# Keys and two values ahead of the score folds: a new order for the weight folding that opens a decoder trunk

## Chip, cores and metric

The kernel runs on one core of a Trainium2 chip. The metric is the device time of one execution in microseconds; the time before is 2403.75 us, the median of three runs (2400.74 to 2407.68).

## What is computed

One layer of a hybrid decoder trunk on x (2048 tokens x 1024 channels, f32) and a memory of 256 tokens, then a final norm:

```
mem_n = rmsnorm(mem, mem_norm_g)
h = rmsnorm(x, mix_norm_g);  q, k, v, g, u = split(h @ w_in)
y_ret  = silu(g) * head_rmsnorm(retention(rope(q), rope(k), v))
y_pool = pool_mixer(u, pool_w) * pool_scale
x = x + concat(y_ret, y_pool) @ w_out
K, V = split(mem_n @ wkv)                 # 4 heads of 256 channels, 256 tokens
x = x + softmax((rmsnorm(x) @ wq) @ K.T / 16) @ V @ wo
x = x + ffn(rmsnorm(x))                   # gated, causal convolution of width 3
out = rmsnorm(x, final_norm_g)
```

The memory has only 256 tokens, so the kernel folds weights before it touches x: `wq` with the keys (a score matrix per head), the values with `wo`, and `pool_w` with the pool's rows of `w_out`. These folds and the norm statistics of the first half of x make up the opening, the first 119 us or so. The change lies there.

## The kernel before

**Numbers.** f32 operands are split in two f32r parts, high (ACT, L264, or L267 with a gain) and low (DVE, L248 or L256), and each product is three matmuls: high x high, high x low, low x high (`passes`, L276 to L278). A weight tile of 128 x 1024 costs one DMA of 512 KB, one ACT pass and one DVE pass before PE can use it.

**The steps of the opening** (`folded_weights`, L430) are traced in the order of the table at L622:

- K 0 to 7 (`keys`, L521) and V 0 to 7 (`memory_values`, L535) each load one tile of `wkv` and project the memory with it (`project`, L499): 8 blocks of 128 channels x 3 passes = 24 matmuls of 256 columns. Two tiles share one PSUM bank. After every second V the bank is split into the value parts (`parted`, L509). A key bank must first be multiplied by the memory's inverse root mean square (`scaled_keys`, L514).
- That scale comes from `memory_norm` (L487), called behind the third key tile: squares on ACT, sums on DVE, four small matmuls over the partitions (`stats`, L350, L357), three Newton steps on DVE for the reciprocal root (`rsqrt`, L300), then `spread` (L365): DVE multiplies an identity by the two parts of the result, PE multiplies by ones (L381), and ACT copies the product to SBUF (L386), so that each column holds its token's scale.
- M 0 to 3 (`score_weights`, L551) fold two rows of `wqT` with two key parts: 4 banks x 2 columns x 2 rows x 3 passes = 48 matmuls; ACT evicts and its queue writes `Md`.
- O 0 to 3 (`output_weights`, L572) fold two rows of `wo` with the values into `VWd`; W 0 to 3 (`pool_weights`, L600) fold the pool weights into `WPd`. Their matmuls have 512 columns.

**Beside them** the loop at L2086 counts the steps n and places the eight tiles of x (`load_x_wide`, L647: load, split, square, add to `total`), the statistics of x (`rows_norm`, L2007, at n = 21, behind O2) and the four loads of value weights (`value_weights`, L726), which the `values` stage reads afterwards.

**What sets the order.** Instructions are traced in program order; a planner with a timing model then orders each engine's queue, the earlier traced first among those that it takes to be ready. `keep_in_program_order` pins an instruction behind the one traced before it on its engine; `issue_after(ins)` pins what its block traces on ins's engine behind ins. On the chip each queue runs strictly in its order. PE has five PSUM banks named `mm`.

**Places.** Raw weights land in a ring of nine places of 512 KB (`raws`, L2083: three in R, two in S, four in Z); a load takes the place that was left longest ago and waits until its last reader is done. `total` holds one such place (R) until `rows_norm` frees it, and memory two until the statistics have read them. Split weights go round a ring of five places (`wides`, L439: Q, two in E, two in G). `other_places` (L441) exchanges two of them behind M3 for the keys' region and four behind V7 for the memory's. SP issues all the loads in one queue.

Of the kernel before, what the change touches and what calls it, by code (L numbers as in the profile page):

```python
# [20 lines left out]
NMEM = 256  # L21
# [121 lines left out]
def trunk(ctx, tc, xT, memT, pos, w_qkgu, w_v, wkv, wqT, wo, wout_r, wout_p, poolT, w_up, w_dn, vecs, consts, outT):  # L143
    nc = tc.nc
    pe, act, dve, pool, sp = nc.tensor, nc.scalar, nc.vector, nc.gpsimd, nc.sync
# [14 lines left out]
    def new_e(at, dtype):  # L160
        return Arena(cp.tile([P, 2 * T], dtype, tag=f"E{at}", name=nm("E")), 0, 2, T)
# [14 lines left out]
    raws = Places([(R, j * T) for j in range(3)] + [(r, 0) for r in S], T)  # L176
# [41 lines left out]
    ones = cp.tile([P, P], F32R, tag="ones", name="ones")  # L218
# [19 lines left out]
    def aux():  # L238
        if both[0] and next(turns_) % 3 == 2:
            return single()  # L240
        return auxp.tile([P, SUB], F32, tag="aux", name=nm("aux"))

    def small(n=4):
        t = smp.tile([P, 8], F32, tag="sm", name=nm("sm"))
        return t[:, :n]

    def tt(eng, out, a, b, op):
        return eng.tensor_tensor(out=out, in0=a, in1=b, op=op)  # L248
# [9 lines left out]
    def bcast(v, n):  # L258
        return v.rearrange("p (a o) -> p a o", o=1).to_broadcast([P, v.shape[1], n])
# [20 lines left out]
    def new_raw():  # L280
        r = raws.take()
        r.free()
        return r.f
# [30 lines left out]
    behind, under, fetched = [iter(())], [iter(())], [None]  # L314
    turned, chained = [], []
    latest, summed = [None], [None]
# [33 lines left out]
    def stats(sums, more=None):  # L350


        cols = [ap[:, t * P : (t + 1) * P] for ap in sums for t in range(ap.shape[1] // P)]
        n = len(cols)
        ps = aux()
        for t, ap in enumerate(cols):
            pe.matmul(ps[:, t : t + 1], ap, one, start=True, stop=more is None)  # L357
            if more is not None:
                pe.matmul(ps[:, t : t + 1], more[:, t * P : (t + 1) * P], one, start=False, stop=True)
        v, y = small(n), small(n)  # L360
        ts(dve, v, ps[:, :n], 1.0 / D, ALU.mult, EPS, ALU.add)
        rsqrt(y, v)
        return y

    def spread(y, outs, keep=True, late=False):  # L365

        yh = smp.tile([P, 8], F32R, tag="yh", name=nm("yh"), bufs=1)[:, : y.shape[1]]
        yl = small(y.shape[1])
        dve.tensor_copy(yh, y)
        tt(dve, yl, y, yh.bitcast(F32), ALU.subtract)  # L370
        at = 0

        one_pair = prs.take() if late else None
        for out in outs:
            n = out.shape[1] // P
            d = one_pair if late else B.take()
            ps = aux()[:, : n * P]
            for i, v in enumerate((yh.bitcast(F32), yl)):
                di = d.r[:, i * SUB : i * SUB + n * P]
                last = tt(dve, di.rearrange("p (a b) -> p a b", a=n), ident.rearrange("p (o b) -> p o b", o=1).to_broadcast([P, n, P]), bcast(v[:, at : at + n], P), ALU.mult)  # L380
                pe.matmul(ps, ones, di, start=i == 0, stop=i == 1)  # L381
            if d is not one_pair or out is outs[-1]:
                d.free()
            if not keep:
                return ps
            act.activation(out, ps, AF.Copy)  # L386
            at += n
        return last
# [41 lines left out]
    def folded_weights():  # L430
# [51 lines left out]
                split(first[:, at], u0[0][:, at], u0[1][:, at], kept="both")  # L482
        rm = TT.take()
        rn = smp.tile([P, 4], F32, tag="rnm", name="rnm", bufs=1)[:, :2]
        bank = []

        def memory_norm():  # L487
            for r in memory:
                tc.keep_in_program_order(act.activation(r.f, r.f, AF.Square))
            f, other = (r.f for r in memory)  # L490
            tt(dve, f, f, other, ALU.add)
            for w in (SUB, NMEM):
                tt(dve, f[:, :w], f[:, :w], f[:, w : 2 * w], ALU.add)
            dve.tensor_copy(rn, stats([f[:, :NMEM]]))
            for r in memory:
                r.free()
            spread(rn, [rm.f[:, :NMEM]], late=True)

        def project(n):  # L499

            u = u0 if n == 0 else wide_pair(second, 2) if n == 1 else wide_pair(load_tile(wkv[n]))
            if n % 2 == 0:
                bank[:] = [mmps()]
            at = n % 2 * NMEM
            ps = bank[0][:, at : at + NMEM]
            for k in range(KT):
                passes(ps, [r[:, k * P : (k + 1) * P] for r in u], (mh[:, k], ml[:, k]), k == 0, k == KT - 1)

        def parted(to, n, ps):  # L509

            hi, lo = (to[:, n - 1 : n + 1, i] for i in range(2))
            split(ps.rearrange("p (n m) -> p n m", n=2), hi, lo)

        def scaled_keys(n, ps):  # L514

            ps3 = ps.rearrange("p (n m) -> p n m", n=2)
            both = rm.f[:, :NMEM].rearrange("p (o m) -> p o m", o=1).to_broadcast([P, 2, NMEM])
            tt(dve, ps3, ps3, both, ALU.mult)
            parted(kp4, n, ps)

        def keys(n):  # L521

            early = bank[0] if n == 2 else None
            project(n)
            if n == 1:
                sp.dma_start(cs_t, consts)
            elif n == 2:
                memory_norm()
                scaled_keys(1, early)
            elif n % 2:  # L530
                scaled_keys(n, bank[0])
            if n == KT - 1:
                rm.free()

        def memory_values(n):  # L535
# [53 lines left out]
        def pool_factors():  # L589

            raw = TT.take()
            r3 = raw.f[:, :SUB].rearrange("p (g c) -> p g c", g=4)
            sp.dma_start(r3, poolT.rearrange("g p c -> p g c"))
            pw = prs.take()
            tt(dve, r3, r3, bcast(pscale, P), ALU.mult)
            split(raw.f[:, :SUB], pw.r[:, :SUB], pw.r[:, SUB:])
            raw.free()
            pool_pair.append(pw)
# [17 lines left out]
        def none_left():  # L616
            mp.free()
            for r in own:
                r.free()

        K, V, M, O, W = keys, memory_values, score_weights, output_weights, pool_weights
        for f, *a in ((K, 0), (K, 1), (K, 2), (K, 3), (K, 4), (K, 5), (M, 0), (K, 6), (M, 1), (K, 7), (V, 0), (M, 2), (V, 1), (V, 2),  # L622
                      (M, 3), (V, 3), (O, 0), (V, 4), (V, 5), (O, 1), (V, 6), (O, 2), (V, 7), (W, 0), (W, 1), (O, 3), (W, 2), (W, 3),
                      (none_left,)):
            f(*a)
            if f is M and a[0] == 3:
                pool_factors()
            yield
# [97 lines left out]
    def value_weights(kp, where=None):  # L726
        raw = new_raw()
        sp.dma_start(raw.rearrange("p (k n) -> p k n", k=2), w_v[2 * kp : 2 * kp + 2].rearrange("k p n -> p k n"))
        u = (B if where is None else B.arenas[where]).take(2)
        for i in range(2):  # L730
            r = raw[:, i * SUB : (i + 1) * SUB]
            split(r, u.r[:, i * T : i * T + SUB], u.r[:, i * T + SUB : (i + 1) * T])
        return u
# [1273 lines left out]
    def rows_norm(s_acc):  # L2007
        rn = smp.tile([P, 8], F32, tag="rn", name=nm("rn"), bufs=3)
        dve.tensor_copy(rn, stats([r.f[:, : r.f.shape[1] // SUB * SUB] for r in s_acc]))
        for r in s_acc:  # L2010
            r.free()
        return rn
# [69 lines left out]
    under[0], spacing[0] = weight_sums(), 2  # L2082
    raws = Places([(R, j * T) for j in range(3)] + [(r, 0) for r in S] + [(Z.arenas[0].t, j * T) for j in range(4)], T)  # L2083
    results = Places([(Z.arenas[1].t, j * T) for j in range(4)], T)
    wv, total, x_at = [], raws.take(), (5, 7, 9, 10, 12, 13, 15, 18)
    for n, _ in enumerate(folded_weights()):  # L2086
        if n in x_at:
            load_x_wide(x_at.index(n), total)
        if n == 21:
            rn = rows_norm([total])  # L2090
        if n in (23, 24):
            wv.append(value_weights(len(wv), 0))
        if n in (25, 26):
            wv.append(value_weights(len(wv), len(wv) - 1))
    rb = [TT.take() for _ in range(NS)]
    normed = (rn, rb)
    behind[0] = spread_steps(rn, [r.f[:, :SUB] for r in rb])
# [1 line left out]
    for b in range(NB):  # L2099

        if b == 0:
            raws = Places([(R, j * T) for j in range(3)] + [(r, 0) for r in S], T)
# [123 lines left out]
        wv, acc, place = [], [], Joined(new_e(0, F32), new_e(1, F32))  # L2226
# [105 lines left out]
    raws = Places([(raws.one[i].t, raws.one[i].base + j * SUB) for i in raws.freed for j in range(2)], SUB)  # L2332
# [116 lines left out]
```

## Time and profile before

| | |
|---|---|
| median of three runs | 2403.75 us |
| the profiled execution | 2400.9 us (span 2399.1, clock 0.996) |
| PE busy, matmuls | 2372.3 us, 11136 |
| DVE, ACT busy | 1796.7, 1386.3 us |
| DMA over the span | 527.78 MB, mean 220 GB/s |
| DMA, on queue q1 | 402.83 MB |

In the profile PE is the matmul engine and PEld its weight loads; DVE, ACT, POOL and SP are the other engines, and a q behind a name is that engine's queue. "L381 <- DVE Q" says that the instruction of line 381 waited for DVE to write tile Q. A helper's line stands for all its callers (L248 is every two-operand DVE operation), so the tiles tell them apart. Matmuls overlap, so the distance between two starts, not the duration, is what one costs. The views by stages give busy time in a stretch, and beside it the clock that TensorE was granted, where 1.00 is full.

### The profile page before, as it was taken

The page shows a single profiled execution, that of the slowest core. Times are in us where ns is not written, and L with a number is a line of the kernel's source. Part 1 is how long each engine was busy: PE and PEld are TensorE (multiplying, and loading weights), DVE is VectorE, ACT ScalarE, POOL GpSimd, SP SyncE. Part 2 cuts the span into 40 slices and gives each one's busy share as a digit, 9 for nine tenths or more (in the row PEclk, how much of TensorE's full clock was granted, in tenths as well). Part 3 has the DMA queues.
Part 4 walks back from the last instruction along what each step waited for, and adds up shares of the span by engine and source line. Part 5 has one row for each costly group of instructions (what it writes and reads, how often), then busy time and mean ns, then how long its engine had stood idle before and what let it go on. Part 6 is the DMA issues. An engine that isn't in the chain of part 4 may idle for free.

```text
span 2399.1 us, 33436 instructions
## 1 busy us (share of the span) xinstructions
PE 2372.3 (99%) x11136; PEld 1981.9 (83%) x11136; DVE 1796.7 (75%) x2977; ACT 1386.3 (58%) x2507; POOL 340.6 (14%) x524
## 2 busy tenths in 40 slices
PE   8999999999999999999999999999999999999998
PEld 7888888888888888888888888888888888888886
DVE  6777776785767777776788776987677698867875
ACT  6754654564445545546555555855555577666663
POOL 0055554454041000000001000110000000000000
PEclk9999999999999999999999999999999999999999
DMA  8899999999585234577578564765456489768951
GB/s 292 303 277 302 283 266 290 297 291 315 191 234 142 74 116 151 172 251 243 168 229 264 180 188 133 254 201 174 157 174 190 132 258 313 237 184 283 342 176 73
DMA packets 269453, 527.78 MB, mean 220 GB/s; under 512 B 30048, under 2 KB 50912, under 8 KB 269280
## 3 DMA queue, kind: packets, MB, share of 16 engines
q1 hardware_dynamic: 212176, 402.83, 51.1%
q0 software_dynamic: 40960, 94.40, 16.5%
q10 hardware_dynamic: 16144, 28.43, 3.2%
q8 instruction: 87, 1.43, 0.2%
q14 instruction: 86, 0.70, 0.1%
HBM read 423.30 MB, written 196.61 MB: 258 GB/s over the span
## 4 chain that ended last, share of the span: by engine, by line
PE 92%; DMA 3%; DVE 3%; ACT 1%; issue 1%; SPq 0%; ACTq 0%; DVEq 0%
PE mm L276 28%; PE mm L278 28%; PE mm L277 28%; PE aux L276 1%; PE aux L278 1%; PE aux L277 1%; PE aux L799 1%; PE aux L773 1%; PE aux L784 1%; PE aux L946 1%; PE aux L801 1%; PE aux L357 0%; DMA WPd<-Z 0%; DVE Z L248 0%; DMA S<-w_v 0%
## 5 line engine op out<-in xcount | busy, mean ns | idle before, releaser
L276 PE MATMUL mm<-G,Q 128*128 128x512 f32 (+1 forms) x1445 | 559.0, 388 | 1.8 <-ACT T L1788 0.5
L277 PE MATMUL mm<-G,Q 128*128 128x512 f32 (+1 forms) x1445 | 558.7, 387 | 0.2 <-DVE G L256 0.2
L278 PE MATMUL mm<-G,Q 128*128 128x512 f32 (+1 forms) x1445 | 555.9, 387 | 1.0 <-DVE Q L248 1.0
L277 PE MATMUL mm<-G,E 128*128 128x512 f32 (+1 forms) x1072 | 410.4, 383 | 1.6 <-DVE G L248 1.6
L276 PE MATMUL mm<-G,E 128*128 128x512 f32 (+1 forms) x1072 | 409.2, 383 | 2.7 <-ACT G L264 2.3
L278 PE MATMUL mm<-G,E 128*128 128x512 f32 (+1 forms) x1072 | 408.9, 383 | 0.4 <-DVE E L248 0.2
L276 PEld LDWEIGHTS mm<-G,Q 128*128 128x128 f32 x1445 | 271.5, 188 | 57.6 <-ACT T L1788 1.0
L278 PEld LDWEIGHTS mm<-G,Q 128*128 128x128 f32 x1445 | 271.5, 188 | 55.4 <-DVE Q L248 1.4
L277 PEld LDWEIGHTS mm<-G,Q 128*128 128x128 f32 x1445 | 271.7, 188 | 54.1 <-DVE G L256 0.4
L248 DVE TENSOR_TENSOR Z<-Z,mm 128x512 f32<-128x512 f32 (+1 forms) x290 | 193.6, 672 | 91.6 <-PE mm L278 89.4
L256 DVE SCALAR_TENSOR_TENSOR Z<-Z,vecs,Z 128x1024 f32<-128x1024 f32 x176 | 224.7, 1280 | 50.1 <-ACT Z L1218 45.5
L276 PEld LDWEIGHTS mm<-G,E 128*128 128x128 f32 x1072 | 202.2, 189 | 42.8 <-ACT G L264 2.6
L277 PEld LDWEIGHTS mm<-G,E 128*128 128x128 f32 x1072 | 202.3, 189 | 40.8 <-DVE G L248 1.9
L278 PEld LDWEIGHTS mm<-G,E 128*128 128x128 f32 x1072 | 202.3, 189 | 40.1 <-DVE E L248 1.0
L248 DVE TENSOR_TENSOR Q<-R,Q 128x512 fp32r<-128x512 f32 (+2 forms) x205 | 140.1, 684 | 81.9 <-ACT Q L1155 48.4
L248 DVE TENSOR_TENSOR T<-T 128x512 f32<-128x512 f32 (+4 forms) x196 | 134.0, 690 | 26.4 <-ACT T L423 12.4
L1155 ACT ACTIVATE Q<-R 128x512 fp32r<-128x512 f32 (+1 forms) x123 | 75.7, 616 | 128.5 <-PE mm L277 119.9
L1155 ACT ACTIVATE E<-R 128x512 fp32r<-128x512 f32 (+1 forms) x163 | 100.3, 615 | 70.9 <-PE mm L277 56.1
L1218 ACT ACTIVATE Z<-Z,vecs 128x1024 f32<-128x1024 f32 x88 | 109.2, 1242 | 37.8 <-DVE Z L248 36.9
L1102 ACT ACTIVATE G<-T 128x512 fp32r<-128x512 f32 x180 | 108.2, 623 | 32.7 <-DMA T<-Gd 24.3
L248 DVE TENSOR_TENSOR Q<-S,Q 128x512 fp32r<-128x512 f32 (+2 forms) x113 | 77.1, 683 | 39.9 <-ACT Q L1155 30.1
L1155 ACT ACTIVATE Q<-S 128x512 fp32r<-128x512 f32 (+1 forms) x81 | 49.9, 616 | 95.5 <-PE mm L277 93.7
(425 smaller groups left out, 4428.9 us busy)
## 6 DMA issues: line engine op xcount, KB each, us to landing
T<-Gd SPq DMA_DIRECT2D x168, 256.0 KB, 4.4
Ud<-w_up POOLq DMA_DIRECT2D x132, 256.0 KB, 9.7
Gd<-Z SPq DMA_DIRECT2D x110, 256.0 KB, 2.7
R<-Ud SPq DMA_DIRECT2D x104, 256.0 KB, 2.7
R<-w_up SPq DMA_DIRECT2D x82, 256.0 KB, 2.9
S<-Ud SPq DMA_DIRECT2D x72, 256.0 KB, 2.8
Gd<-T SPq DMA_DIRECT2D x56, 256.0 KB, 3.4
T<-Xd SPq DMA_DIRECT2D x53, 256.0 KB, 4.4
```

What stands on the lines that cost most here:

```text
L248: return eng.tensor_tensor(out=out, in0=a, in1=b, op=op)
L256: return dve.scalar_tensor_tensor(out=out, in0=a, scalar=s, in1=b, op0=op0, op1=op1)
L276: pe.matmul(ps, lh, rh, start=start, stop=False, skip_group_check=more)
L277: pe.matmul(ps, lh, rl, start=False, stop=False, skip_group_check=more)
L278: latest[0] = pe.matmul(ps, ll, rh, start=False, stop=stop, skip_group_check=more)
L773: pe.matmul(col(sc, c), self.ch(k, c), self.ch(q, c), start=True, stop=True)
L784: pe.matmul(col(kv, c), col(self.kn.f, c), self.ch(v, c, h * T), start=True, stop=True)
L799: pe.matmul(col(y, c), col(self.pr.f, c), self.ch(v, c, h * T), start=True, stop=self.cur[c] is None)
L801: pe.matmul(col(y, c), self.ch(q, c), self.cur[c], start=False, stop=True)
L1102: one = act.activation(hi, x, AF.Copy, scale=-1.0 if i == 2 else 1.0)
L1155: act.activation(p2[:, 0, :w], self.raw[i].f[:, :w], AF.Copy)
L1218: act.activation(self.c[g].f, a[:, 2:], AF.Identity, bias=cb[:, f : f + 1], scale=cw[2][:, f : f + 1])
```

## The change

1. The table of steps: K6 and K7 come directly behind K5, then V0 and V1, and from there score folds alternate with values (M0, V2, M1, V3, M2, V4, M3). Before, M0 and M1 stood between K5, K6 and K7, and M2 behind V0.
2. `memory_norm` still runs behind K2 but no longer spreads its result. The spread moves behind the last key, its two matmuls pinned behind the last matmul of K7 (`behind`), and all four key banks are scaled there instead of each behind its second tile.
3. The steps at which x's tiles and the value weights are placed change with the table. The last two value weights now come together behind W3.
4. `total.back = None`: when the sum of x's squares is freed, its place does not go back into the ring of raw places.

```diff
-    def spread(y, outs, keep=True, late=False):
+    def spread(y, outs, keep=True, late=False, behind=None):
...
-                pe.matmul(ps, ones, di, start=i == 0, stop=i == 1)
+                with tc.issue_after(behind) if behind is not None else nullcontext():
+                    pe.matmul(ps, ones, di, start=i == 0, stop=i == 1)
...
-        bank = []
+        bank, done = [], []
...
-            spread(rn, [rm.f[:, :NMEM]], late=True)
...
-            early = bank[0] if n == 2 else None
             project(n)
             if n == 1:
                 sp.dma_start(cs_t, consts)
             elif n == 2:
                 memory_norm()
-                scaled_keys(1, early)
-            elif n % 2:
-                scaled_keys(n, bank[0])
+            if n % 2:
+                done.append((n, bank[0]))
             if n == KT - 1:
+                spread(rn, [rm.f[:, :NMEM]], late=True, behind=latest[0].ins)
+                for pair in done:
+                    scaled_keys(*pair)
                 rm.free()
...
-        for f, *a in ((K, 0), (K, 1), (K, 2), (K, 3), (K, 4), (K, 5), (M, 0), (K, 6), (M, 1), (K, 7), (V, 0), (M, 2), (V, 1), (V, 2),
-                      (M, 3), (V, 3), (O, 0), (V, 4), (V, 5), (O, 1), (V, 6), (O, 2), (V, 7), (W, 0), (W, 1), (O, 3), (W, 2), (W, 3),
+        for f, *a in ((K, 0), (K, 1), (K, 2), (K, 3), (K, 4), (K, 5), (K, 6), (K, 7), (V, 0), (V, 1), (M, 0), (V, 2), (M, 1), (V, 3),
+                      (M, 2), (V, 4), (M, 3), (O, 0), (V, 5), (O, 1), (V, 6), (O, 2), (V, 7), (W, 0), (W, 1), (O, 3), (W, 2), (W, 3),
                       (none_left,)):
...
-    wv, total, x_at = [], raws.take(), (5, 7, 9, 10, 12, 13, 15, 18)
+    wv, total, x_at = [], raws.take(), (5, 7, 8, 9, 11, 13, 16, 18)
     for n, _ in enumerate(folded_weights()):
         if n in x_at:
             load_x_wide(x_at.index(n), total)
         if n == 21:
+            total.back = None
             rn = rows_norm([total])
-        if n in (23, 24):
+        if n in (24, 25):
             wv.append(value_weights(len(wv), 0))
-        if n in (25, 26):
-            wv.append(value_weights(len(wv), len(wv) - 1))
+        if n == 27:
+            wv += [value_weights(kp, kp - 1) for kp in (2, 3)]
```

## The prediction

> **What bounds the kernel now.** I began with the page's busy times.
>
> ```profile
> span 2399.1 us, 33436 instructions
> PE 2372.3 (99%) x11136; PEld 1981.9 (83%) x11136; DVE 1796.7 (75%) x2977; ACT 1386.3 (58%) x2507; POOL 340.6 (14%) x524
> ```
>
> TensorE (PE) is busy all but 26.8 us, so only time in which it stands still or runs slowly can be saved. The view by stages shows where that is; its columns are start:end, length, then busy time (and instructions) of PE, PEld, DVE, ACT, POOL, then granted clock, share of the DMA engines and GB/s.
>
> ```profile
> 0.00:119.00 119.00, 104.27 (x713) 96.79 (x714) 82.82 (x121) 85.75 (x115) 0.20 (x4) 0.96 0.84 297
> 20.00:25.90 5.90, 5.90 (x50) 5.73 (x49) 4.15 (x8) 2.71 (x3) 0.00 (x0) 1.00 1.03 402
> 25.90:31.00 5.10, 0.04 (x2) 0.01 (x1) 4.82 (x16) 1.53 (x2) 0.00 (x0) 0.90 1.03 410
> 31.00:40.10 9.10, 5.20 (x20) 4.56 (x21) 6.98 (x11) 6.83 (x10) 0.00 (x0) 0.50 0.39 156
> 36.60:40.10 3.50, 3.49 (x16) 3.49 (x17) 2.38 (x4) 1.90 (x3) 0.00 (x0) 0.50 0.00 0
> 113.00:116.00 3.00, 2.98 (x12) 2.17 (x13) 3.00 (x6) 1.88 (x4) 0.00 (x0) 1.00 0.53 171
> 130.00:300.00 170.00, 169.58 (x821) 142.25 (x820) 134.46 (x254) 92.07 (x211) 99.71 (x154) 1.00 1.04 284
> 135.00:2399.10 2264.10, 2252.06 (x10356) 1872.28 (x10354) 1706.57 (x2847) 1293.35 (x2380) 339.17 (x519) 1.00 0.70 215
> ```
>
> The opening (the folds, to about 119 us) holds 119.0 - 104.3 = 14.7 us of the idle time, the 2264 us behind it only 12.0. Between 31.0 and 40.1 us PE also ran at half its clock. Third came PE's timeline (start, duration; in brackets how long PE stood before the row, and for whom).
>
> ```profile
> 25.54 0.28 PE L277 MATMUL mm<-G,Q 128*128 128x256 f32 x1
> 25.66 0.28 PE L278 MATMUL mm<-G,Q 128*128 128x256 f32 x1
> 31.00 0.92 PE L381 MATMUL aux<-Q,ones 128*128 128x256 f32 x2 [5.06 <-DVE Q L248]
> 34.26 0.80 PE L276 MATMUL mm<-G,E 128*128 128x256 f32 x2 [2.34 <-ACT G L264]
> 36.61 0.58 PE L277 MATMUL mm<-G,E 128*128 128x256 f32 x1 [1.56 <-DVE G L248]
> ...
> 37.21 0.41 PE L276 MATMUL mm<-G,E 128*128 128x256 f32 x1
> 37.42 0.41 PE L277 MATMUL mm<-G,E 128*128 128x256 f32 x1
> ...
> 43.80 0.28 PE L276 MATMUL mm<-G 128*128 128x256 f32 x1
> ...
> 113.02 0.72 PE L276 MATMUL mm<-Q 128*128 128x512 f32 x2 [2.53 <-ACT Q L264]
> ```
>
> At 25.66 PE ends the sixth key tile (K5). The next in its queue is the spread of the memory norm (L381), which waits 5.06 us for DVE, and behind that M0, the first score fold, which needs the scaled keys that the spread leads to: 2.34 us for their high half (ACT), 1.56 us for the low (DVE). K6 starts only at 43.80. Starts are 0.12 us apart at full clock (25.54 to 25.66) and 0.21 at half (37.21 to 37.42). From 25.66 to 43.80 are 18.14 us, whose work is one last key matmul, two of the spread and 48 of M0 (4 banks, 2 columns, 2 rows, 3 passes): 51 x 0.12 = 6.1 us. The stall costs 12.0 us.
>
> The chain behind it is in DVE's timeline (the last two rows: scaling three banks by the spread, then their low halves).
>
> ```profile
> 23.36 0.16 DVE L253 TENSOR_SCALAR sm<-aux 128x2 f32<-128x2 f32 x1 [0.99 <-PE aux L357]
> 23.85 1.23 DVE L248 TENSOR_TENSOR E<-S,E 128x1024 fp32r<-128x1024 f32 x1 [0.33 <-ACT E L264]
> ...
> 30.86 0.42 DVE L248 TENSOR_TENSOR Q<-consts,sm 128x256 fp32r<-128x256 f32 x1
> ...
> 32.88 1.89 DVE L248 TENSOR_TENSOR mm<-mm,T 128x512 f32<-128x512 f32 x3
> ...
> 35.87 1.88 DVE L248 TENSOR_TENSOR G<-mm,G 128x512 fp32r<-128x512 f32 x3
> ```
>
> The reciprocal root takes from 23.36 to 31.28 although its pieces last 0.16 us: 1.23 us splits stand between them.
>
> **The change, part by part.** *Keys first.* A key or value tile is 24 matmuls, 2.88 us at 0.12. With K6 and K7 directly behind K5, PE has work from 25.7 to 31.5, and the spread is pinned behind it; its inputs are there at 31.28 by the row above. V0 and V1 then cover the way to the scaled keys until 37.7; that way took from 31.00 to about 36.6 before. M0 ends near 43.5, where now K6 would only begin; K6, K7, V0 and V1 (11.5 us) have moved into the hole. Removed: 12.0 us.
>
> What is late next? (a) If one more 1.2 us split falls into the root's chain, the spread waits: 0 to 2 us, taken at 1.0, since the margin is 31.5 - 31.3. Everything on PE stands behind that wait. (b) A fourth bank is now scaled ahead of M0 (0.63 + 0.63 us of DVE by the x3 rows), with x's work between: 0 to 1, taken at 0.5. Of the five banks four hold keys meanwhile; V0 and V1 use the fifth, so PE isn't held for a bank before M0. (c) Loads. SP's queue before:
>
> ```profile
> 8.26 0.33 SPq L473 DMA_DIRECT2D S<-wqT  x1
> 12.92 0.33 SPq L473 DMA_DIRECT2D S<-wqT  x1
> ...
> 29.37 0.33 SPq L651 DMA_DIRECT2D Z<-xT  x1
> 41.32 0.33 SPq L473 DMA_DIRECT2D R<-wqT  x1
> ...
> 101.47 0.40 SPq L728 DMA_DIRECT2D S<-w_v  x1
> 107.54 0.34 SPq L473 DMA_DIRECT2D R<-wout_p  x1
> ```
>
> ```profile
> Z<-wkv SPq DMA_DIRECT2D x11, 512.0 KB, 6.9
> 24.04 1.06 ACT L264 ACTIVATE G<-Z 128x1024 fp32r<-128x1024 f32 x1 [0.22 <-DMA Z<-wkv]
> ```
>
> K6 and K7 take over the raw places and moments of M0's two rows (8.26, 12.92), so they are split by 12.92 + 6.9 + 1.06 + 1.23 = 22.1, well ahead. V0 is the tight one. Counting the ring of raw places through the new order, its load falls to a place that memory held until the sum of squares is read (just ahead of 23.36). Landing takes 6.9 us, ACT's split 1.06, DVE's 1.23: about 32.3 against 31.8. 0 to 3 us, taken at 1.0, for the transfers were full then (share 1.03). (d) The tail. At 113.02 the first pool fold (W0) waited 2.53 us because its split place was the one V7 had just left. In the new order M3 swaps places two takes later, the ring turns, and W0's place is left by O2, ahead of V7. Then W1 waits for V7 instead, behind W0's 6 matmuls of twice the columns (6 x 0.24 = 1.4 us). 0 to -2.5, taken at -1.4. (e) Total kept out of the ring: SP stood from 101.47 to 107.54 because W2's load wanted total's place. PE had other work in that time, so nothing. The value weights that move behind W3 are read only behind O3 (24 matmuls), W2 and W3 (12) and half of the first values group (24): 60 x 0.24 = 14 us, against a landing of 6.9 and two splits: nothing; uncovered they would cost that landing. x's tiles move by one to three steps. No matmul of the folds reads them, but their splits are pinned in ACT's queue with fold splits behind them; if x's load is late these wait too, which I leave in the 3 us of (c).
>
> Sum: -12.0 + 1.0 + 0.5 + 1.0 - 1.4 = -10.9 us; the ends are -14.5 and -6.0. Against the profiled execution (2400.9 us, 1.8 of it outside the span) that is 2390.0. The median of the three runs is 2403.75, 2.85 above the profiled one; the saving is the same for both, so I predict **2392.9**, and 2389.3 to 2397.8 for this case.
>
> Two more rows set the reserves. Full transfers move 402 to 410 GB/s here, and the opening moves 297 over 119 us, 35.3 MB: 88 us at 402, where the shortened opening has 107. The Trainium skill ("DMA: Bandwidth & Descriptors", Specifications) gives some 358 GB/s as the limit from HBM per core; by it the same bytes would need an estimated 99 us, and I would give the load rival below 0.3 in place of 0.2. The trace goes above that figure, so I keep 402.
>
> After the 5.06 us wait, half clock lasts through 3.5 us of unbroken work (36.6 to 40.1), a loss of 1.7; after the 2.53 us wait the clock is full (113 to 116). So the sum, whose waits are at most 3 us, has no term for the clock, and the rivals with longer waits have 1.7. "TensorE: Matmul & The Clock Gate" in the Trainium skill (Part 1) puts the limit at an idle window of about 3.4 us; both waits here agree, and by it a wait of 3 us at V0 is just short of the price.
>
> **The rivals.** *The wait comes back as a load.* Between 29.37 and 41.32 SP issued nothing: the next load wanted a place that an x tile still held until ACT and DVE were through with it. It cost nothing, as PE was itself behind. If x1 is as slow in the new order, PE has in hand V0, V1, M0 and V2 to about 46.4, and M1's second row, issued 1.3 us (0.524 MB at 402 GB/s) behind 41.3, is split at 42.6 + 6.9 + 1.06 + 1.23 = 51.8: a wait of 5.4, with 1.7 for the clock. 12.0 - 7.1 = 4.9 saved: 2398.9. For it: x's loads keep their order on SP. Against: ACT was blocked then by the very spread wait that goes. Chance 0.2.
>
> *The change doesn't do all it says.* The planner orders by its own times. If it holds V0 for late and issues M0 behind the spread, PE waits from 31.8 to 37, as now, once: 5.2 + 1.7, 5.1 saved: 2398.7. Chance 0.1; the edges pin only the spread.
>
> *Slower.* Between 8.26 and 29.37 SP issued seven loads that the new order asks for only behind V1 (five rows for score folds, two x tiles; the first and last rows are above). If these 7 x 0.524 = 3.7 MB stay in arrears to the end of the opening, they meet the stretch from 130 to 300 us, whose transfers are full (1.04) at 284 GB/s: 12.9 us of waiting, and PE, idle 0.4 us there now, would lose them and 1.7 to the clock: 2403.75 - 12.0 + 14.6 = 2406. It decides from (12.0 - 1.7) x 0.284 = 2.9 MB of arrears on. Against: the opening's reserve of 107 - 88 us. Chance 0.05.
>
> **How the numbers follow.** The forecast has 0.65. A measurement of this kernel tells about 0.3% (7.2 us) from no change. The forecast's range lies beyond that but for its weak end (0.58 of 0.65), and the two middle rivals reach it if their waits are half as long (0.06 of 0.3). Faster 0.64, same 0.31, slower 0.05. The range takes in the forecast's own and the two middle rivals: 2389 to 2401.
>
> **What would show it.** Right: L381 behind the eighth key tile with a wait under 2 us, PE's clock at 1.00 from 10 us on, the opening some 11 us shorter, and the wait ahead of W0 gone or moved to W1. Wrong: a PE wait over 3.4 us at L381, at V0 or at M1, a silence on SP around 30 to 40 us with PE waiting at its end, or more than 12.0 us idle behind the opening.

## The result, and the profile after

The changed kernel takes 2389.53 us (median of five runs, 2388.79 to 2391.31) against 2400.74 for the kernel before, measured beside it (the three runs known so far and two more, 2399.7 to 2407.68). The ratio is 0.9948 [0.9933, 0.9963]: 11.2 us or 0.5% faster. The forecast of 2392.9 stood on a median before of 2403.75; its saving of 10.9 is within 0.3 us of the measured one. The terms behind that number are another matter, as the rows show. One execution behind the medians below stands out, 4860.77 us in the run with x's tiles later, and the ratios leave it out. First the busy times of the page:

```profile
span 2387.8 us, 33436 instructions
PE 2368.7 (99%) x11136; PEld 1980.8 (83%) x11136; DVE 1796.6 (75%) x2977; ACT 1385.8 (58%) x2507; POOL 337.9 (14%) x524
```

PE stands for 19.1 us where it stood for 26.8. That is 7.7 of the 11.3 us by which the span shrank; the other 3.6 are busy time. 2.4 of these lie ahead of the first pool fold, where fewer matmuls run at half clock; the traces don't say what the other 1.2 are. The view by stages of the kernel after has the columns of the prediction's fence:

```profile
0.00:119.00 119.00, 111.00 (x751) 102.75 (x752) 88.45 (x128) 90.10 (x124) 0.20 (x4) 0.99 0.93 327
31.00:40.10 9.10, 6.84 (x58) 6.63 (x56) 8.01 (x10) 8.10 (x12) 0.00 (x0) 1.00 0.59 188
40.40:42.00 1.60, 1.59 (x13) 1.60 (x14) 1.60 (x4) 1.60 (x2) 0.00 (x0) 1.00 0.94 312
58.00:60.00 2.00, 2.00 (x11) 2.00 (x11) 2.00 (x3) 0.97 (x2) 0.00 (x0) 0.50 1.04 393
140.00:300.00 160.00, 160.00 (x796) 135.14 (x795) 120.86 (x232) 84.55 (x196) 91.18 (x140) 1.00 1.05 285
```

Between 31.0 and 40.1 us 58 matmuls are recorded at full clock, where it was 20 at half. The stretch from 140 to 300 us has no idle time at all; it will matter below. PE's timeline after shows the spread, the two waits that are left, the first pool fold (W0), and two small waits behind it:

```profile
31.69 0.40 PE L382 MATMUL aux<-Q,ones 128*128 128x256 f32 x2
40.41 0.35 PE L276 MATMUL mm<-G,Q 128*128 128x256 f32 x1 [2.57 <-DVE G L248]
56.36 0.39 PE L276 MATMUL mm<-G 128*128 128x256 f32 x1 [2.78 <-ACT G L264]
103.49 0.63 PE L276 MATMUL mm<-Q 128*128 128x512 f32 x2
105.23 0.73 PE L276 MATMUL mm<-G,Q 128*128 128x512 f32 x2 [0.19 <-ACT G L264]
106.20 0.50 PE L276 MATMUL mm<-G 128*128 128x512 f32 x1 [0.23 <-ACT Z L611]
```

The spread (L382 now) stands behind K7 and waits for nothing. V0 and V1 follow without a wait. W0 begins at 103.49, not at 113.02, and its wait is gone. M0 waits 2.57 us at 40.41. DVE's timeline says for what: the four key banks are multiplied, then come the splits of two weight tiles (M0's second row and V2's tile), then the banks' low halves.

```profile
34.91 2.49 DVE L248 TENSOR_TENSOR mm<-mm,T 128x512 f32<-128x512 f32 x4
37.31 2.35 DVE L248 TENSOR_TENSOR E<-S,E 128x1024 fp32r<-128x1024 f32 x2
39.58 2.48 DVE L248 TENSOR_TENSOR G<-mm,G 128x512 fp32r<-128x512 f32 x4
```

M0's first matmul (L276) needs only high halves, and it still waited for a low one. The low split is the last reader of the first key bank, so the first matmul lacked a PSUM bank: four held keys, and the fifth V0 and V1. But the second matmul (L277, at 40.60) multiplies by the low half itself, so a free bank alone would have started one matmul earlier and no more. What M0 waits for is the low half, which DVE makes behind the two weight tiles.

The other wait, 2.78 us at 56.36, is M1's second row. Its load shows in SP's queue, and its split in ACT's:

```profile
48.60 0.33 SPq L474 DMA_DIRECT2D R<-wqT  x1
```

```profile
55.25 1.06 ACT L264 ACTIVATE G<-R 128x1024 fp32r<-128x1024 f32 x1 [0.33 <-DMA R<-wqT]
```

The load was issued at 48.60, when DVE had added up an x tile and so freed its place; ACT was waiting for the data at 55.25, 6.65 us later. This is the load rival's place and mechanism, at about 0.6 of its price.

### The profile page after: what moved, and what is told of

The parts are those of the page before. It is cut to its first block, busy times and chain, and to the rows that moved or that the text cites. A ratio compares the mean times of both kernels' runs of the same rounds, so it can differ in the third digit from the quotient of the medians.

```text
span 2387.8 us, 33436 instructions
## 1 busy us (share of the span) xinstructions
PE 2368.7 (99%) x11136; PEld 1980.8 (83%) x11136; DVE 1796.6 (75%) x2977; ACT 1385.8 (58%) x2507; POOL 337.9 (14%) x524
## 4 chain that ended last, share of the span: by engine, by line
PE 97%; DMA 1%; DVE 1%; ACT 0%; issue 0%; SPq 0%; DVEq 0%; ACTq 0%
PE mm L276 30%; PE mm L278 30%; PE mm L277 30%; PE aux L276 1%; PE aux L278 1%; PE aux L277 1%; PE aux L800 1%; PE aux L774 1%; PE aux L785 1%; PE aux L947 1%; PE aux L802 1%; PE aux L357 0%; DMA S<-w_v 0%; DVE Z L248 0%; DMA Xd<-E 0%; PE aux L776 0%
## 5 line engine op out<-in xcount | busy, mean ns | idle before, releaser
L276 PE MATMUL mm<-G,Q 128*128 128x512 f32 (+1 forms) x1445 | 558.4, 388 | 4.3 <-DVE G L248 2.6
L277 PE MATMUL mm<-G,Q 128*128 128x512 f32 (+1 forms) x1445 | 558.7, 387 | 0.2 <-DVE G L256 0.2
L277 PE MATMUL mm<-G,E 128*128 128x512 f32 (+1 forms) x1072 | 409.4, 382 | 0.0
L276 PE MATMUL mm<-G,E 128*128 128x512 f32 (+1 forms) x1072 | 408.3, 382 | 0.3 <-DVE Z L248 0.3
L276 PEld LDWEIGHTS mm<-G,Q 128*128 128x128 f32 x1445 | 271.4, 188 | 60.2 <-issue 2.7
L277 PEld LDWEIGHTS mm<-G,Q 128*128 128x128 f32 x1445 | 271.5, 188 | 54.4 <-DVE G L248 0.4
L276 PEld LDWEIGHTS mm<-G,E 128*128 128x128 f32 x1072 | 201.4, 188 | 39.7 <-DVE Z L248 0.8
L277 PEld LDWEIGHTS mm<-G,E 128*128 128x128 f32 x1072 | 201.5, 188 | 38.9
L248 DVE TENSOR_TENSOR Q<-S,Q 128x512 fp32r<-128x512 f32 (+1 forms) x112 | 75.9, 678 | 38.8 <-ACT Q L1156 30.1
```

The source lines that it names most:

```text
L276: pe.matmul(ps, lh, rh, start=start, stop=False, skip_group_check=more)
L277: pe.matmul(ps, lh, rl, start=False, stop=False, skip_group_check=more)
```

## The experiments

The first two theories: (A) the saving is the PE work that now fills the wait for the norm's root, and the rest of the change only keeps out of its way; (B) and (C) put part of it down to the places of the loads, or to the late, pinned spread. The pin could not be told apart: without it every queue has the same instructions in the same order. Theory (D), that the saving reaches the end only if the next stage's first x tile can load early, came out of the first results. Each ratio is to runs of the kernel before taken beside it.

**Total's place back in the ring.** The kernel after without one line:

```diff
         if n == 21:
-            total.back = None
             rn = rows_norm([total])
```

> The changed kernel, but total's place goes back into the ring of raw places when it is freed, as before. Theory A (the saving is PE work put into the wait for the norm's root; the places matter only where PE waits for a load): W2's load waits again for total's place behind O2, PE has other work by then; 2389 to 2391 us. Rival B (the saving comes from loads that no longer stand in SP's queue): at least 3 us are lost, 2393 us or more.

It took 2403.56 us, ratio 1.001 [1.0001, 1.0018]: nothing is left of the saving. Theory (A), 2389 to 2391, failed; (B) forecast a loss of at least 3 us, but not what makes it. The opening is not the reason. The first pool fold's eviction starts at 103.44 us there, 2.1 earlier than in the kernel after (105.56), as M1's second row doesn't wait there. The loss comes later. By stages, then on PE's timeline:

```profile
140.00:300.00 160.00, 149.47 (x719) 123.69 (x718) 119.77 (x230) 80.40 (x187) 90.44 (x142) 0.98 1.05 278
```

```profile
159.91 0.50 PE L276 MATMUL mm<-G,Q 128*128 128x512 f32 x1 [0.92 <-ACT Q L1774]
162.17 0.50 PE L278 MATMUL mm<-G,Q 128*128 128x512 f32 x1 [1.53 <-DVE Q L248]
...
198.02 0.80 PE L278 MATMUL mm<-G,Q 128*128 128x512 f32 x1 [5.71 <-DVE Q L248]
```

PE stands for 10.5 us in a stretch where the kernel after has none. Follow it back through SP's queue (issue time, and how long the group took, waits between its loads included):

```profile
98.59 0.33 SPq L474 DMA_DIRECT2D R<-wout_p  x1
99.01 0.77 SPq L1638 DMA_DIRECT2D R<-xT  x1
107.14 28.90 SPq L1638 DMA_DIRECT2D R<-xT  x5
```

and DVE's:

```profile
112.17 1.22 DVE L248 TENSOR_TENSOR G<-R,G 128x1024 fp32r<-128x1024 f32 x1
...
120.98 0.69 DVE L248 TENSOR_TENSOR R<-R 128x512 f32<-128x512 f32 x1 [6.39 <-ACT T L1650]
...
194.26 2.50 DVE L248 TENSOR_TENSOR Z<-Z,T 128x512 f32<-128x512 f32 x4 [5.15 <-DMA Z<-rope_d]
...
197.28 0.68 DVE L248 TENSOR_TENSOR Q<-S,Q 128x512 fp32r<-128x512 f32 x1
```

W2's row takes total's place (R0) at 98.59, but DVE reads it for the last time at 112.17. The next stage starts its own ring of places with R0, so its x tiles (`quarter_sums`, L1638) queue behind that reader. DVE stands 6.39 us for the first of them, until 120.98; in the kernel after the same instruction starts at 117.98, although PE is 2 us later. From there every load slips: the rope tables come so late that DVE waits 5.15 us for them at 194.26, and behind that instruction in DVE's queue stands the split (197.28) for which PE waits 5.71.

**The spread back in `memory_norm`.** The kernel after with its table, but the spread called and each key bank scaled where the kernel before did it, unpinned:

```diff
+            spread(rn, [rm.f[:, :NMEM]], late=True)
...
-                for pair in done:
-                    scaled_keys(*pair)
+            elif n % 2:
+                scaled_keys(n, bank[0])
```

> The changed kernel's table of steps, x places and ring, but the norm is spread inside memory_norm and the key banks are scaled each behind its second tile, as before; no pin on the spread. Theory A: with K6 and K7 ready ahead of it the spread is queued behind them anyway, so the table alone carries the saving: 2389 to 2392 us, no wait over 1 us at the spread. Rival C (the late spread and its pin are what saves): PE meets the spread early again, a wait of about 5 us and half clock return: 2396 us or more.

2395.39 us, ratio 0.9973 [0.9963, 0.9982]. That fits neither forecast: about half of the saving is there without the late spread, so (A)'s table alone doesn't carry it, and (C) is wrong about the cause, because on PE the spread still stands behind K7 with no wait of 5 us. What differs is the order on ACT and DVE: right behind the spread PE waits 1.55 and 0.76 us, with the clock at 0.50 from 34.82 to 38.23, and a later wait of 2.98 (until 58.23) has the same effect.

**No values ahead.** M0 directly behind the keys:

```diff
-(K, 6), (K, 7), (V, 0), (V, 1), (M, 0), (V, 2), (M, 1), (V, 3), (M, 2), (V, 4), (M, 3),
+(K, 6), (K, 7), (M, 0), (V, 0), (M, 1), (V, 1), (M, 2), (V, 2), (V, 3), (V, 4), (M, 3),
```

> The changed kernel with V0 and V1 not ahead of M0: M0, V0, M1, V1, M2, V2, V3, V4, M3 behind the keys; the swap of split places stays at the same take. Theory A: PE stands between the spread and M0 for the way to the scaled keys, 5.6 us (before) to 8.4 us (in the changed kernel, 32.0 to 40.4) less what else is ready, in place of 2.6, and runs at half clock after it: 2393 to 2397 us. Rival B: the values ahead do not matter, 2389 to 2391 us.

2395.05 us, ratio 0.9971 [0.9961, 0.9982]: the two values are worth about half of the saving, as (A) has it. PE's timeline there (the traced execution took 2400.57):

```profile
36.81 0.58 PE L276 MATMUL mm<-G 128*128 128x256 f32 x1 [5.14 <-ACT G L264]
39.74 0.58 PE L277 MATMUL mm<-G 128*128 128x256 f32 x1 [2.35 <-DVE G L248]
```

This also shows what a bank is worth to M0. With the fifth bank free, M0's first matmul starts on the high half (ACT), and the second (L277) still waits for the low half, until 39.74. The bank holds back one matmul, the low half all the others.

**The kernel before without the norm's root.** It leaves out the memory's statistics and root (the scale is 1), so that nothing waits for them:

```diff
-            dve.tensor_copy(rn, stats([f[:, :NMEM]]))
+            dve.memset(rn, 1.0)
```

> The kernel before, in its old order, with the memory's statistics and reciprocal root left out: the scale is set to 1. Theory A: the spread no longer waits, M0 starts behind K5, the stall of 12.0 us goes nearly whole, the clock stays at 1.00: 2389 to 2392 us. Rival B: the old order of loads stays, so at most 3 us are saved: 2397 us or more.

2400.25 us, ratio 0.9991 [0.9983, 1.0]: theory (A) alone failed here, and (B) has the time. W0 starts at 103.82, 9.2 us ahead of the kernel before, and then the gain is given back. PE's timeline and ACT's:

```profile
119.86 0.80 PE L276 MATMUL mm<-G,Q 128*128 128x512 f32 x1 [6.52 <-ACT Z L610]
```

```profile
119.21 0.60 ACT L610 ACTIVATE Z<-mm 128x512 f32<-128x512 f32 x1 [5.99 <-DMA WPd<-Z]
```

PE doesn't wait for an x tile here. It waits for an eviction of the pool folds (L610), and that one for the store of an earlier pool fold (`WPd`) to leave its place. The stretch from 140 to 300 us has no idle time in this run (160.00 busy). The same kernel with `total.back = None` as well:

> The old order with the memory's statistics and root left out (scale 1), and total's place out of the ring. Its twin with total in the ring had its first pool fold at 103.8 us, 9.2 ahead of the kernel before, and gave all of it back by 121 us. Theory D: with R0 free the stage behind starts earlier; 5 to 10 us are kept, 2390 to 2396 us. Rival F (what was given back was a store of the pool folds that the evictions wait for, apart from R0): no more than 2 us are kept, 2398 us or more.

2392.63 us, ratio 0.9958 [0.9945, 0.997]. 1.19 us is left of the 6.52, and the eviction hardly waits for the store:

```profile
115.08 0.50 PE L276 MATMUL mm<-G,Q 128*128 128x512 f32 x1 [1.19 <-ACT Z L610]
```

```profile
114.43 0.60 ACT L610 ACTIVATE Z<-mm 128x512 f32<-128x512 f32 x1 [0.17 <-DMA WPd<-Z]
```

The time is theory (D)'s, so the line is worth 7.6 us in the old order too, once PE is early. The wait that it takes away there is the one that rival (F) named, a store, and not the first x tile; (F) was wrong that the line has no part in it. Why the store is late with the place in the ring, these runs don't show; W2's load and the x tiles behind it are issued at other times.

**That line alone**, added to the kernel before:

> The kernel before with one line more: total's place stays out of the ring of raw places. Theory D (the opening's saving reaches the end only if the first x tile of the stage behind, which lands in the same place R0, is loaded earlier too; total out of the ring does that): PE waits for nothing there in the old order, so alone the line saves 0 to 1.5 us: 2399 to 2402. Rival E (the line is the saving, whatever the order): 2389 to 2393 us.

2404.68 us, ratio 1.0013 [1.0003, 1.0024]: alone it saves nothing, which refutes (E); the time is even above the 2399 to 2402 of (D). In the kernel before PE stood for only 0.4 us between 130 and 300 us (169.58 of 170.00 busy), so there was no such wait to take away. So neither the order nor the line saves anything without the other.

**R0 last.** If the late reader of R0 is the cause, total may go back into the ring as long as the next stage doesn't begin with R0. The kernel after with two edits:

```diff
-            total.back = None
...
-            raws = Places([(R, j * T) for j in range(3)] + [(r, 0) for r in S], T)
+            raws = Places([(R, j * T) for j in (1, 2)] + [(r, 0) for r in S] + [(R, 0)], T)
```

> The changed kernel with total's place back in the ring (so W2's row lands in R0, as in the run that lost the saving), but the ring of the stage behind begins with R1 and ends with R0, so its first x tile does not wait for W2's row. Theory D: most of the saving comes back, 2389 to 2394 us. Rival G (W2's late load itself, or the transfers behind it, cost the time): 2398 us or more.

2390.61 us, ratio 0.9949 [0.9935, 0.9963]: the whole saving is back. DVE reads W2's row as late as before, yet the first x tile doesn't wait for it, and the stretch behind has no idle time. DVE's timeline and the stage:

```profile
112.33 1.22 DVE L248 TENSOR_TENSOR G<-R,G 128x1024 fp32r<-128x1024 f32 x1
...
115.40 0.69 DVE L248 TENSOR_TENSOR R<-R 128x512 f32<-128x512 f32 x1 [0.65 <-ACT T L1650]
```

```profile
140.00:300.00 160.00, 160.00 (x800) 135.25 (x799) 121.90 (x235) 85.81 (x198) 95.81 (x139) 1.00 1.05 277
```

That is theory (D), shown for the new order by the order of the ring alone.

**x's tiles later**, to move them off the way to M0:

```diff
-x_at = (5, 7, 8, 9, 11, 13, 16, 18)
+x_at = (5, 9, 10, 11, 13, 15, 17, 18)
```

> The changed kernel with x's second to seventh tile placed later (steps 9, 10, 11, 13, 15, 17 in place of 7, 8, 9, 11, 13, 16). Theory: the two waits left in the opening come from x: its pinned ACT and DVE work stands ahead of the scaled keys (2.57 us at M0), and an x tile holds the raw place of M1's second row (2.78 us). With x later both shrink; the opening is 2 to 5 us shorter, and since the stage behind is tied to the same chain of loads the end gains 0 to 4 us: 2386 to 2390. Rival: the loads of x come too late for the statistics, 2391 us or more.

2398.71 us, ratio 0.9983 [0.9973, 0.9993]: worse than the kernel after. The planner puts the spread later (PE at 35.51), M0 waits 3.52 us, until 42.65, and the clock is 0.50 from 44 to 46; six more waits between 64 and 125 us add 5.5. Fewer x tiles in the way of M0 doesn't mean an earlier M0.

**The spread between K6 and K7.** Can the 2.57 us before M0 be had too? K7's matmuls are pinned behind the spread, and the first three banks are scaled there:

```diff
-            if n == KT - 1:
+            if n == KT - 2:
                 spread(rn, [rm.f[:, :NMEM]], late=True, behind=latest[0].ins)
-                for pair in done:
-                    scaled_keys(*pair)
+                while done:
+                    scaled_keys(*done.pop(0))
+            if n == KT - 1:
+                scaled_keys(*done.pop())
```

> The kernel after, with the spread put between K6 and K7 on PE (K7's matmuls behind it) and the first three key banks scaled there. Tells what M0's 2.57 us wait in the kernel after is. If it is the late spread, which lets the first key bank free its PSUM place only with the low part at 39.58: DVE multiplies the banks some 3 us earlier, the wait of 2.57 before M0 goes, and PE stands about 1.3 us before the spread instead (root's second product ends at 29.66, K6 at 28.82); span 0.5 to 2 us shorter than after's, 2387 to 2389.5. If the wait is M0's own (four key banks and the values' bank hold all five whatever the scale does), it stays at 2 us or more and the new 1.3 comes on top: 2390 to 2392.

2390.43 us, ratio 0.9957 [0.9944, 0.9969], the same as the kernel after. The wait at M0 did go, and without the 1.3 us ahead of the spread. PE then runs on into the next late load. Its timeline, and ACT's:

```profile
54.95 0.36 PE L276 MATMUL mm<-G,E 128*128 128x256 f32 x1 [4.01 <-DVE G L248]
```

```profile
50.60 1.15 ACT L267 ACTIVATE G<-Z,vecs 128x1024 fp32r<-128x1024 f32 x1 [2.75 <-DMA Z<-xT]
51.66 1.04 ACT L264 ACTIVATE Q<-R 128x1024 fp32r<-128x1024 f32 x1
52.60 0.58 ACT L264 ACTIVATE G<-mm 128x512 fp32r<-128x512 f32 x1
```

ACT waits 2.75 us for an x tile, and the split of a value bank stands two places behind it in ACT's queue. PE is going again at 54.95, where it was at 56.36: of the 2.57 us gained, 1.4 outlast the transfers, and half clock follows here too (0.50 from 55.38 to 58.79). W0 still starts 1.4 us earlier than in the kernel after, at 102.05. The traced execution took 2394.46 and loses that again in a wait of 3.71 us at 440.32, far behind the change; where the faster executions lose it isn't shown. With both edits, this one and R0 last:

> The same with total's place back in the ring and R0 at the end of the next stage's ring. With total back the load of M1's second row has a place that is free and its 2.78 us wait goes (it was 0.2 there before), so with both edits PE should stand under 2 us between 31 and 107 us. If waits in the opening reach the end one for one, 2384 to 2388; if they are given back behind 300 us, 2389 to 2391, the same as after.

2391.39 us, ratio 0.9956 [0.9942, 0.997]. PE waits 3.94 us at the same step. The expectation that PE would stand under 2 us failed, and no version here beats the kernel after.

## Why the prediction was right in its size and wrong in a step

**The stall, -12.0: right.** The matmuls of K6, K7, V0 and V1 run through from 25.7 to 37.7 at full clock, as forecast.

**(a) The spread's wait, forecast 1.0: 0.** DVE had the spread's last input ready at 29.66, 2 us before PE came to it.

**(b) The fourth bank, forecast 0.5: 2.57.** The mis-sized part is DVE's way from the spread to the first low half. PE went on with that half 5.6 us behind the spread in the kernel before (31.00 to 36.61) and 8.7 behind it in the kernel after (31.69 to 40.41), 3.1 more where the term allowed 0.5. The splits of M0's second row and of V2's tile, 2.35 us at 37.31, stand ahead of it; the term counted the fourth bank and x's work, and not these. "PE isn't held for a bank before M0" is wrong as well: it counted who holds banks while V0 and V1 run, and not that M0 then needs a sixth. But that costs one matmul, as the run without values ahead shows.

**(c) Loads, forecast 1.0 at V0: 0 there, about 4.3 at M1.** V0 didn't wait: its tile was loaded at 17.11 us, and the place that memory held went to V1's (23.50). M1's second row did wait, 2.78 us, and the clock was half from 56.69 to 60.10, an estimated 1.5 us more (3.4 us at starts 0.21 apart in place of 0.12). By the same reckoning the 1.7 that the prediction charges for 3.5 us of half clock is 1.5. That "the sum, whose waits are at most 3 us, has no term for the clock" failed with it.

**(d) W0, forecast -1.4: -2.1.** Its 2.53 went, and two waits of 0.19 and 0.23 came behind it, in place of the 1.1 put there for W1.

**(e) "Total kept out of the ring ... nothing": this is the step that failed.** It looked only at whom W2's late load kept waiting then, and found PE busy. It did not ask who takes that place next. With PE 10 us ahead, the next stage's first x tile wants R0 while W2's row still lies in it. Without the line the time is 2403.56 and not 2389.53, 14 us, more than the whole saving; by the prediction's terms that kernel would also have been at 2392.9. The forecast hit its size because the change held the line that its working counted at nothing.

**The sum.** Ahead of W0 both kernels have the same 688 matmuls. The views of before and after up to W0:

```profile
0.00:113.02 113.02, 98.30 (x688) 92.16 (x688) 78.04 (x113) 81.26 (x109) 0.20 (x4) 0.95 0.85 302
0.00:103.49 103.49, 95.91 (x688) 91.26 (x689) 74.21 (x103) 76.65 (x102) 0.20 (x4) 0.98 0.92 325
```

PE stood for 14.7 us in the first and for 7.6 in the second, and was busy 2.4 us less: 9.5 in all, by which W0 starts earlier. The measured terms give -12.0 + 2.6 + 4.3 - 2.5 = -7.6, and -1.0 for a wait at 72.25 us in the kernel before that the prediction had left out: -8.6; the last 0.9 is in no single wait above 0.4 us. So (b) and (c) cost 6.9 where 1.5 were forecast. Of the prediction's signs for being right, two failed: the opening is 9.5 us shorter and not 11, and the clock isn't 1.00 throughout from 10 us on. A further 1.8 come between W0 and the end of the span, 0.6 of them idle time, and stay open. That the sum came out within 0.3 us of the measured saving is luck.

**The rivals.** The planner did not put M0 behind the spread. The load rival happened, at M1 as it said, for 2.78 + 1.5 us and not for 5.4 + 1.7. The slower rival had the place right (the full transfers between 130 and 300 us), and nearly the price: 2406, where the run with total back gave 2403.56 and 10.5 us of waiting. Its cause was wrong. Not megabytes in arrears but one place with a late reader made the stage wait, and the one line of the change that the working passed over took that away.

## What to carry to other kernels

A saved wait in one stage is only kept if the next stage can begin earlier by as much: look for what its first load waits for, and for who reads that place last, before counting an edit of a ring at nothing. When a saving disappears, compare the idle time of the stages behind the change and not only the change's own. When a step's inputs are said to be ready, ask for both halves of a split: here the high half was there 3 us before the low one, and the second matmul needs the low one.

## What the runs showed of the hardware

No single length of wait decides here whether TensorE keeps its clock. After 2.57 us it stayed at 1.00 in the kernel after (40.41) and fell to 0.50 in the kernel with R0 last (40.82); after 2.53 us it was 1.00 in the kernel before (113.02), and after 1.55 and 0.76 us, close together, 0.50 in the run with the spread back in `memory_norm`. The Trainium skill ("TensorE: Matmul & The Clock Gate", Part 1) puts the limit at an idle window of about 3.4 us; the length recurs here, but the falls above came with shorter waits. In these traces the half clock sets in on a raster of 3.41 us that is fixed within a run, and lasts for whole steps of it, as from 56.69 to 60.10. Two steps of R0 last, then three of the kernel after (columns as above):

```profile
37.73:41.14 3.41, 0.84 (x8) 0.67 (x7) 3.41 (x5) 3.41 (x6) 0.00 (x0) 1.00 0.31 119
41.14:44.55 3.41, 3.41 (x19) 3.41 (x18) 3.41 (x6) 2.58 (x4) 0.00 (x0) 0.50 0.57 189
36.21:39.63 3.42, 1.63 (x14) 1.42 (x12) 3.42 (x5) 3.42 (x6) 0.00 (x0) 1.00 0.03 12
39.63:43.04 3.41, 2.63 (x22) 2.66 (x23) 3.41 (x6) 3.10 (x5) 0.00 (x0) 1.00 0.92 282
53.28:56.69 3.41, 0.63 (x5) 0.43 (x4) 1.63 (x2) 2.58 (x3) 0.00 (x0) 1.00 1.04 420
```

In R0 last the whole wait falls into one step, in which PE is busy for 0.84 us, and the next step has half clock. In the kernel after a boundary divides the same wait, PE is busy for 1.63 and 2.63 us, and the clock holds; its wait of 2.78 us lies in one step (0.63 busy), and half clock follows. So the share of a step in which PE stands seems to count, and where the raster lies is luck. No run moved a wait to test that, and it doesn't explain every fall: falls at 9.14 and 108.13 in the run with x later follow steps in which PE is busy for 2.38 and 2.55 us.

While PE stood before 56.36, the transfers moved 418 GB/s (stage 53.50 to 56.30, DMA share 1.04), a little above the 402 to 410 that the prediction worked with.
